# Attention probabilities turned two key tiles at a time: two PSUM banks taken in one run of eight transposes, and split one behind the other

## The chip, the core and the metric

The kernel runs on one core of one Trainium2 chip. A core has five engines with a queue of instructions each: TensorE (PE, matrix products, with the loading of its stationary operand shown apart as PEld), VectorE (DVE), ScalarE (ACT), GpSimd (POOL) and SyncE (SP, which only issues transfers here). They work side by side and wait for one another through semaphores. TensorE writes its results to PSUM, in banks of 2 KB for each of 128 partitions, which VectorE and ScalarE read. The metric is the device time of one execution in microseconds, the median over the runs.

## What is computed

One step of a one-layer streaming encoder on 2048 prompt rows and 64 sample rows of width 1024. One input projection feeds a convolution branch and a banded attention; both are gated, merged, projected, and followed by a feed-forward part. Cut to what matters here:

```python
def conv_module(u, hist, w_dw, b_dw, ln_g, ln_b, w_out):
    ext = jnp.concatenate([hist, u], axis=1)
    y = lax.conv_general_dilated(ext, w_dw[:, None, :], ...)      # 31 taps, 512 channels
    y = jax.nn.silu(layer_norm(y + b_dw, ln_g, ln_b))
    return y @ w_out, ext[:, -(CONV_K - 1):]

def band_attend(q, k, v, q_pos, k_pos, rel_bias):
    s = jnp.einsum('bqhd,bkhd->bhqk', q, k) * ATTN_SCALE
    s = s + rel_bias[:, rel][None]
    s = jnp.where(mask, s, NEG_INF)      # own chunk of 64 and the 8 chunks before it
    p = jax.nn.softmax(s, axis=-1)
    return jnp.einsum('bhqk,bkhd->bqhd', p, v)

def encoder_layer(x, c, conv_hist, attend, p):
    h = rms_norm(x, p['norm1_g']) * (1 + sc1) + sh1
    glu_a, glu_b, q, k, v, g_conv, g_attn = jnp.split(h @ p['w_in'], offs, axis=-1)
    conv_out, conv_state = conv_module(glu_a * jax.nn.sigmoid(glu_b), conv_hist, ...)
    q = rms_norm(q.reshape(B, T, N_HEADS, HEAD_DIM), p['q_norm_g'])
    k = rms_norm(k.reshape(B, T, N_HEADS, HEAD_DIM), p['k_norm_g'])
    attn_out = attend(q, k, v, p['rel_bias']).reshape(B, T, ATTN_DIM) @ p['w_attn_out']
    merged = jax.nn.sigmoid(g_conv) * conv_out + jax.nn.sigmoid(g_attn) * attn_out
    x = x + gt1 * (merged @ p['w_o'])
    h2 = rms_norm(x, p['norm2_g']) * (1 + sc2) + sh2
    gate, up = jnp.split(h2 @ p['w_ffn_in'], 2, axis=-1)
    x = x + gt2 * ((jax.nn.silu(gate) * up) @ p['w_ffn_out'])
    return x, conv_state, k, v
```

There are 8 heads of 64 channels. All data are 32-bit floats.

## The kernel before

**Numbers.** A 32-bit operand is split into a high and a low part that TensorE can take at speed. `split` (L725) is one copy on ScalarE, which makes the high part, and one subtraction on VectorE behind it, which makes the low part, the residue. A product of two split operands is three matmuls (`mm3`, L706). Weights are split in the same way on arrival: `whi` on ScalarE, `wlo` on VectorE or GpSimd.

**Stages.** The rows are cut into four blocks (`PBLOCKS`, L35): block 0 has the 64 sample rows and 512 prompt rows, blocks 1 to 3 have 512 each. For each block the order of stages is q, 0, k, 1, v, 2, 3, g (`ORDER`, L559). q, k and v are the three attention projections (`qkv`, L1200), 0 to 3 are the four channel tiles of the convolution's gated input, each followed by 31 taps on VectorE (`convolve`, L1267), and g is the 16 column tiles of the two gates (`gates`, L1347; with the activation `gate` on ScalarE and a store from ScalarE's queue). The rows of the following block are normalised meanwhile (`norm_tile`, L1172): squares and sums on ScalarE, a power on GpSimd for the reciprocal root, `x_t` on VectorE, and eight transposes on TensorE (`pt<-ident,x_t`). When all four blocks are through, a second phase (from L1692, with PSUM pools of its own) does the merge, the output projection and the feed-forward part.

**The order of the work.** The kernel writes one list of instructions by hand. `Meter` (L85) passes each engine call on and books an estimate of its time to a load per engine in `Stream` (L170); all calls go through one line, so every instruction of the profile says L102 and tiles are told apart by their names. The projections and gates are the main thread. After about each 500 ns of TensorE work by the estimate, `tick` (L211) first does what is due and then gives each `Lane` (L108) a turn. A lane holds generators; a turn runs one of them from one `yield` to the next, and a yielded time says when it may go on by TensorE's estimated clock. The lanes are, in order, `norm_lane` (normalisation), `work` (rows of queries and keys, `qk_rows` L1064), `attn` (attention, at most two heads at a time), `tail` (`conv_norm`, L1289) and `conv` (the taps). `attn` has turns at least `ATTN_NS` = 600 ns apart and none while VectorE's load is over 3000 ns or ScalarE's over 4000 ns ahead of TensorE's (L1608); in block 3 the spacing is 0 and a turn takes two steps. What is left when the last block's gates are through is run out by `attn.drain` (L1684). A scheduler then places the instructions of that list on the engines' queues, where their order is fixed.

**Attention.** `attend(i)` (L1495) is one head of one block. In block 0, heads of the prompt rows and of the sample rows ("s") alternate, and a query tile looks back at up to four key tiles; in the other blocks a query tile has 640 keys (five key tiles). Per head:

- For each of the four query tiles: the score products (`sc<-kk,q`) into the one score tile of PSUM; then `softmax_max` (L1382), which is one VectorE instruction (adds the bias and takes the maximum, `pr<-sc,bias`) and one on ScalarE (exponential and sum, `pr<-pr,sm`); then, a tile late, `softmax_scale` (L1398), a reciprocal on VectorE and a scaling, on ScalarE for every head (`ON_ACT` names all). A tap waits in the order for the last such maximum (`ahead_of_taps`).
- Then for each key tile `jj` in `seq` (L1574 on): up to four transposes `ptp<-ident,pr` into one general PSUM bank, `split` into `ph` and `pl` (three buffers each), a `yield`. The value products `av(jj)` (L1562), which accumulate `po<-ph,vv` and `po<-pl,vv` in the one bank "o", wait in the list `pend` until three key tiles are split, and run before the fourth is turned. The generator yields with a time for each value product, and without one after each key tile.
- Then `finish_head` (L1432): two halves of `po` are added (`o_p` for the prompt rows), and every second head is split and stored.

The general banks are five (`ps_g`, tag "gp", L771); projections, gates, normalisation, the means of the convolution (`pm<-s,ones`) and the transposed probabilities all take them in turn. Two banks hold one tile of scores and one holds `po`, which makes eight in all.

**The convolution's normalisation.** `conv_norm` (L1289) begins when all taps of a block are done: GpSimd adds the four channel tiles to `s`, TensorE multiplies by ones for the mean (first `pm`), VectorE subtracts it, ScalarE squares, GpSimd adds the squares, TensorE multiplies by ones again (second `pm`), and the rest follows on ScalarE, VectorE and GpSimd. In block 0 it is done twice, for the sample rows and for the prompt rows.

Of the kernel before, what the change touches and what calls it, by code (L numbers as in the profile page):

```python
# [8 lines left out]
F32 = mybir.dt.float32  # L9
# [7 lines left out]
P = 128  # L17
# [600 lines left out]
def streaming_layer(ctx: ExitStack, tc: tile.TileContext, I, O):  # L618
    nc = tc.nc
    stream = Stream()  # L620
    pe, dve, act, gps = (
        Meter(e, n, stream) for e, n in ((nc.tensor, "pe"), (nc.vector, "dve"), (nc.scalar, "act"), (nc.gpsimd, "pool"))
    )
# [28 lines left out]
    ident = const.tile([P, P], F32, name="ident")  # L652
# [72 lines left out]
    def split(hi, lo, src):  # L725
        act.activation(hi, src, AF.Copy)
        stream.after("dve", "act")
        dve.tensor_tensor(lo, src, hi.bitcast(F32), ALU.subtract)
# [42 lines left out]
    ps_g = p1.enter_context(tc.tile_pool(name="ps_g", bufs=5, space=PSUM))  # L771
# [626 lines left out]
    def softmax_scale(pr, sm, n, w, on_act):  # L1398
        dve.reciprocal(sm[:n, 3:4], sm[:n, 2:3])
        if on_act:  # L1400
            stream.after("act", "dve")
            act.activation(pr[:n, :w], pr[:n, :w], AF.Copy, scale=sm[:n, 3:4])
        else:
            dve.tensor_scalar(pr[:n, :w], pr[:n, :w], sm[:n, 3:4], None, ALU.mult)
# [48 lines left out]
    def spans(b):  # L1453

        if b == "s":
            return 0, SMP, 0, CACHE + SMP
        past = QB if b else 0
        return SMP + QB * b, QB, CACHE + SMP + QB * b - past, QB + past
# [18 lines left out]
    def fetch_qk(i):  # L1477
        if i < len(order) and ("qk", i) not in now:
            x, h = order[i]
            now["qk", i] = load_qk(x, h, *spans(x))  # L1480

    def fetch(i):
        if i < len(order) and i not in loaded:
            x, h = order[i]
            fetch_qk(i)
            if now["bias"] is None or now["bias"][0] != h:
                now["bias"] = h, load_bias(h)
            loaded[i] = stream.load["pe"] + DMA_LAG

    def fetch_v(i):  # L1490
        if i < len(order) and ("v", i) not in now:
            x, h = order[i]
            now["v", i] = load_v(h, *spans(x)[2:])

    def attend(i):  # L1495
        x, h = order[i]
        q0, nq, k0, nk = spans(x)
        yield lambda: now["scored"] == i - 1
        fetch(i)
        fetch_v(i)  # L1500
        if not i:
            fetch_qk(1)
        yield loaded[i]
        (q2, kk), (_, bias), vnow = now["qk", i], now["bias"], now["v", i]
        tiles = []
        for t in range(0, nq, P):
            n = min(P, nq - t)
            if x not in (0, "s"):
                ps = ps_a.tile([P, 2, 512], F32, tag="s", name="sc")
                for j in range(2):  # L1510
                    for d in range(2):
                        pe.matmul(ps[:, j, :320], q2[:, d, t : t + P], kk[:, t + 320 * j : t + 320 * j + 320], start=d == 0, stop=d == 1)
                w, src, bs = 640, ps[:, :, :320], bias[:, ::-1]
            else:
                w = nk if x == "s" else t + P

                if "banks" not in now:
                    sc = ps_a.tile([P, 2, 512], F32, tag="s", name="sc")
                    now["banks"] = [sc[:, 0:1], sc[:, 1:2]]
                ps = now["banks"].pop(0)  # L1520
                now["banks"].append(ps)
                for d in range(2):
                    pe.matmul(ps[:n, 0, :w], q2[:, d, t : t + n], kk[:, :w], start=d == 0, stop=d == 1)
                src, bs = ps[:n, 0:1, :w], bias[:n, 64:384][:, ::-1] if x == "s" else bias[:, :w][:, ::-1]
            pr, sm, free, ready = softmax_max(src, n, w, bs)
            tiles.append((pr, sm, n, w))
            if t + P < nq:
                yield free + PE_LAG, SCORE_ROOM
            else:
                fetch(i + 1)  # L1530
                if (x, order[min(i + 2, len(order) - 1)][0]) in ((0, 0), ("s", "s")):
                    fetch_qk(i + 2)
                now["scored"] = i
            if t:
                softmax_scale(*tiles[-2], x in ON_ACT)
        yield ready
        softmax_scale(*tiles[-1], x in ON_ACT)
        yield stream.when("act" if x in ON_ACT else "dve") + PE_LAG
        while now["finished"] < i - 1:
            yield lambda: now["finished"] == i - 1  # L1540
        fetch_v(i + 1)
        po = ps_a.tile([P, 512], F32, tag="o", name="po")
        if x == "s":
            pt = ps_g.tile([P, 512], F32, tag="gp", name="ptp")
            ph = wk.tile([P, 512], F32R, tag="ph", name="ph", bufs=3)
            pl = wk.tile([P, 512], F32R, tag="pl", name="pl", bufs=3)
            js = ((0, P), (1, P), (2, SMP))
            for j, m in js:
                c = slice(j * SMP, j * SMP + SMP)
                pe.transpose(pt[:m, c], tiles[0][0][:SMP, j * P : j * P + m], ident[:SMP, :SMP])  # L1550
            stream.after("act", "pe")
            split(ph[:, : 2 * SMP], pl[:, : 2 * SMP], pt[:, : 2 * SMP])
            split(ph[:SMP, 2 * SMP : 3 * SMP], pl[:SMP, 2 * SMP : 3 * SMP], pt[:SMP, 2 * SMP : 3 * SMP])
            yield stream.when("dve") + PE_LAG
            for j, m in js:
                c = slice(j * SMP, j * SMP + SMP)
                for y_ in (ph, pl):
                    pe.matmul(po[:, :SMP], vnow[:m, j], y_[:m, c], start=j == 0 and y_ is ph, stop=j == 2 and y_ is pl)
        else:
            seq = (0, 1, 2, 3) if x == 0 else (3, 4, 0, 1, 2)  # L1560

            def av(jj, ph, pl, _):  # L1562
                if x:
                    uses = [(jj, 0, min(jj, 3) + 1)] + ([(jj + 5, jj + 1, 4)] if jj < 3 else [])
                else:
                    uses = [(jj, jj, 4)]
                for j, a, e in uses:
                    for y_ in (ph, pl):
                        pe.matmul(
                            po[:, a * P : e * P], vnow[:, j], y_[:, a * P : e * P], start=jj == seq[0] and y_ is ph,  # L1570
                            stop=jj == seq[-1] and y_ is pl and j == uses[-1][0], skip_group_check=True,
                        )

            pend = []  # L1574
            for jj in seq:
                if len(pend) > 2:
                    yield pend[0][3] + PE_LAG
                    av(*pend.pop(0))
                pt = ps_g.tile([P, 512], F32, tag="gp", name="ptp")
                t0 = 0 if x else jj  # L1580
                for t in range(t0, 4):
                    j = (jj - t + (5 if t > jj else 0)) if x else jj
                    pe.transpose(pt[:, t * P : t * P + P], tiles[t][0][:, j * P : j * P + P], ident)
                ph = wk.tile([P, 512], F32R, tag="ph", name="ph", bufs=3)
                pl = wk.tile([P, 512], F32R, tag="pl", name="pl", bufs=3)
                stream.after("act", "pe")
                w = 512 - t0 * P
                if x in ON_POOL and jj % 2:
                    p32 = temp("p32")
                    act.activation(p32[:, :w], pt[:, t0 * P :], AF.Copy)  # L1590
                    act.activation(ph[:, t0 * P :], p32[:, :w], AF.Copy)
                    stream.after("pool", "act")
                    gps.tensor_tensor(pl[:, t0 * P :], p32[:, :w], ph[:, t0 * P :].bitcast(F32), ALU.subtract)
                    pend.append((jj, ph, pl, stream.when("pool")))
                else:
                    split(ph[:, t0 * P :], pl[:, t0 * P :], pt[:, t0 * P :])
                    pend.append((jj, ph, pl, stream.when("dve")))
                yield
            for args in pend:
                yield args[3] + PE_LAG  # L1600
                av(*args)
        yield stream.when("pe")
        yield from finish_head(h, po, SMP if x == "s" else QB, q0, "s" if x == "s" else "p")
        now["finished"] = i
# [87 lines left out]
    ps_g = ctx.enter_context(tc.tile_pool(name="ps_c", bufs=4, space=PSUM))  # L1692
# [184 lines left out]
    for s, (lo, hi) in enumerate(CBLOCKS):  # L1877
        tiles = token_tiles(lo, hi)
# [476 lines left out]
```

## Time and profile before

| | |
|---|---|
| Median of 3 runs | 2961.91 us (2960.33 to 2962.21) |
| The profiled execution | 2958.2 us, with a span of 2956.1 us |
| Mean granted TensorE clock | 0.996 |
| TensorE busy before the first attention | 158.48 of 173.00 us |
| TensorE busy from the first attention to the end of the first phase | 987.41 of 1017.00 us (173 to 1190) |
| TensorE busy behind it | 1749.66 of 1766.00 us |

The span runs from the first instruction to the last. The attention's own groups of instructions, with their count, busy time and mean:

| Engine, instruction | count | busy us | mean ns |
|---|---|---|---|
| TensorE, scores `sc<-kk,q` | 448 | 91.1 | 320 |
| TensorE, turned probabilities `ptp<-ident,pr` | 584 | 89.9 | 272 |
| TensorE, values `po<-ph,vv` and `po<-pl,vv` | 248 each | 75.1 each | 313, 320 |
| ScalarE, exponential and scaling `pr<-pr,sm` | 272 | 200.2 | 747 |
| ScalarE, copy `ph<-ptp` | 168 | 87.2 | 533 |
| VectorE, maximum `pr<-sc,bias` | 136 | 97.9 | 720 |
| VectorE, residue `pl<-ptp,ph` | 168 | 100.0 | 606 |

Busy means that an instruction was in execution; a TensorE that waits for an operand between two matmuls is idle. A matmul's own duration overlaps those of its neighbours (272 ns for a transpose is from its start to its modelled end), so its price in time is read from the distance of starts. In a row of a timeline, the columns are start and duration in us, engine, line, operation, output and inputs by name, sizes, and how many such instructions stand in a run; a bracket gives the idle time in front and what ended it. In a table of windows each engine has its busy time and, in brackets, the number of its instructions, and then follow the granted clock of TensorE as a share of the full one, the busy share of the transfer engines, and GB/s.

### The profile page before, as it was taken

To read this page: it belongs to the slowest core of one execution; us is meant where nothing else is said; L and a number is where in the kernel's file an instruction comes from. 1 tells how busy PE (TensorE), PEld (TensorE's weight loads), DVE (VectorE), ACT (ScalarE), POOL (GpSimd) and SP (SyncE) were. 2 spreads that over 40 slices of the span, in tenths; PEclk is the share of its full clock that TensorE was granted. 3 is DMA by queue.
4 is the path that set the end of the run, shared out by engine and by line. 5 is a ranking of instruction groups with operands and counts; after the bars stand their busy time and mean duration, and the time that the engine had idled before them with its cause. 6 is when DMAs were issued, how large, how long until landed. Compare 5 with 4: busy or idle time off the path is not lost.

```text
span 2956.1 us, 44848 instructions
## 1 busy us (share of the span) xinstructions
PE 2895.5 (98%) x16193; PEld 2587.1 (88%) x16193; DVE 2041.9 (69%) x3648; ACT 1363.3 (46%) x2453; POOL 1166.4 (39%) x753
## 2 busy tenths in 40 slices
PE   8999899999999999999999999999999999999999
PEld 5899777787888788888999998999999999999998
DVE  5897687668857885577777746676666547566666
ACT  3345633661465257464433345444444345444442
POOL 1101310111011103454566452366667742465767
PEclk9999999999999999999999999999999999999999
DMA  9988889988987889985444776332333965333333
GB/s 320 320 291 293 285 277 299 286 260 275 303 277 221 277 248 286 280 293 172 150 152 146 261 256 228 99 118 93 114 122 104 332 223 185 97 96 111 115 107 126
DMA packets 467066, 628.04 MB, mean 212 GB/s; under 512 B 36196, under 2 KB 314584, under 8 KB 466845
## 3 DMA queue, kind: packets, MB, share of 16 engines
q1 hardware_dynamic: 452944, 606.11, 63.1%
q10 hardware_dynamic: 13901, 19.08, 1.8%
q8 instruction: 127, 2.08, 0.3%
q14 instruction: 94, 0.77, 0.1%
HBM read 476.53 MB, written 148.54 MB: 211 GB/s over the span
## 4 chain that ended last, share of the span: by engine, by line
PE 48%; DVE 2%; ACT 1%; issue 1%; DMA 0%; POOL 0%; ACTq 0%; DVEq 0%
PE ps L102 29%; PE pd L102 14%; PE pw L102 5%; DVE wlo L102 1%; DVE pw L102 0%; ACT whi L102 0%; DVE ps L102 0%; DVE t L102 0%; DMA tg<-g_d 0%; DVE sums L102 0%; PE pt L102 0%; DVE acc L102 0%; ACT xn L102 0%; DVE hid L102 0%; ACT hid L102 0%
## 5 line engine op out<-in xcount | busy, mean ns | idle before, releaser
L102 PE MATMUL ps<-t,whi 128*128 128x384 f32 (+1 forms) x2112 | 501.7, 322 | 3.0 <-DVE u L102 0.9
L102 POOL TENSOR_TENSOR wlo<-wst,whi 128x1024 fp32r<-128x1024 f32 (+1 forms) x159 | 363.7, 2298 | 243.3 <-ACT whi L102 231.0
L102 ACT ACTIVATE whi<-wst 128x1024 fp32r<-128x1024 f32 (+1 forms) x265 | 258.3, 979 | 321.8 <-PE ps L102 135.0
L102 PE MATMUL ps<-b,whi 128*128 128x384 f32 (+1 forms) x1584 | 381.6, 326 | 6.4 <-ACT early L102 2.7
L102 PEld LDWEIGHTS ps<-t,whi 128*128 128x128 f32 x2112 | 367.7, 188 | 10.2 <-ACT u L102 3.3
L102 DVE SCALAR_TENSOR_TENSOR y<-u,wd,y 128x512 f32<-128x512 f32 (+1 forms) x480 | 369.3, 773 | 6.3
L102 PE MATMUL ps<-hh,whi 128*128 128x512 f32 (+2 forms) x992 | 361.6, 365 | 0.0
L102 DVE TENSOR_TENSOR acc<-acc,pd 128x512 f32<-128x512 f32 x482 | 322.2, 684 | 48.5 <-PE pd L102 46.0
L102 PE MATMUL ps<-hl,whi 128*128 128x512 f32 (+2 forms) x992 | 345.6, 348 | 0.0
L102 PE MATMUL ps<-hh,wlo 128*128 128x512 f32 (+2 forms) x992 | 345.1, 348 | 0.0
L102 PE MATMUL ps<-t,wlo 128*128 128x384 f32 (+1 forms) x1056 | 338.2, 321 | 0.0
L102 PE MATMUL pd<-whi,hid 128*128 128x512 f32 x912 | 297.2, 391 | 0.3 <-DVE hid L102 0.3
L102 PEld LDWEIGHTS ps<-b,whi 128*128 128x128 f32 x1584 | 278.0, 189 | 14.5 <-ACT early L102 4.1
L102 POOL TENSOR_TENSOR r<-t,mhalf 128x1 f32<-128x1 f32 (+2 forms) x68 | 84.1, 1244 | 444.5 <-DVE t L102 434.2
L102 PE MATMUL ps<-b,wlo 128*128 128x384 f32 (+1 forms) x792 | 256.8, 324 | 0.0
L102 ACT ACTIVATE pr<-pr,sm 128x640 f32<-128x640 f32 (+3 forms) x272 | 200.2, 747 | 111.8 <-DVE sm L102 109.2
L102 PEld LDWEIGHTS ps<-hh,wlo 128*128 128x128 f32 x992 | 186.7, 188 | 21.7
L102 PEld LDWEIGHTS ps<-hh,whi 128*128 128x128 f32 x992 | 187.1, 189 | 18.6 <-issue 1.9
L102 DVE TENSOR_TENSOR wlo<-wst,whi 128x1024 fp32r<-128x1024 f32 (+1 forms) x106 | 135.1, 1277 | 98.7 <-ACT whi L102 97.2
L102 PEld LDWEIGHTS pd<-whi,hid 128*128 128x128 f32 x912 | 171.1, 188 | 36.2 <-ACT hid L102 0.7
L102 PEld LDWEIGHTS ps<-hl,whi 128*128 128x128 f32 x992 | 187.5, 189 | 15.5 <-issue 1.4
L102 PEld LDWEIGHTS ps<-t,wlo 128*128 128x128 f32 x1056 | 198.1, 188 | 0.8
(233 smaller groups left out, 6297.4 us busy)
## 6 DMA issues: line engine op xcount, KB each, us to landing
whi<-w_din_h SPq DMA_DIRECT2D x72, 512.0 KB, 6.7
wlo<-w_din_l SPq DMA_DIRECT2D x72, 512.0 KB, 7.5
wst<-sum_d SPq DMA_DIRECT2D x131, 256.0 KB, 2.9
wfo<-in_w_ffn_out SPq DMA_DIRECT2D x64, 512.0 KB, 4.1
wmod<-in_w_ada SPq DMA_DIRECT2D x46, 512.0 KB, 9.0
sum_d<-ws SPq DMA_DIRECT2D x88, 256.0 KB, 2.0
wst<-in_w_ffn_in SPq DMA_DIRECT2D x85, 256.0 KB, 3.3
wst<-in_w_in SPq DMA_DIRECT2D x40, 512.0 KB, 7.6
```

Source lines behind the costliest of these rows:

```text
L102: self.last = f(*args, **kw)
```

## The change

One new helper, `turn_probs(jj)`, holds the transposes of one key tile. When the loop comes to a key tile that isn't turned yet, it takes that one and the next in `seq` and turns both, eight transposes in a row into two general banks, and notes the two banks in `turned`. The loop then splits the first, comes round without a `yield`, finds the second turned already, and splits it. So the only `yield` without a time left is the one behind the second of a pair, or behind a last one that stands alone. The rule for the value products changes with it: one runs when more than two tiles are in `pend`, or when exactly two are in it and a pair is about to be turned (not for the last key tile of `seq` on its own).

In blocks 1 to 3 with `seq` = (3, 4, 0, 1, 2) the steps of a head were: turn 3, turn 4, turn 0, value 3 and turn 1, value 4 and turn 2, values 0, 1, 2. Now they are: turn 3 and 4, value 3 and turn 0 and 1, value 4 and turn 2, values 0, 1, 2. In block 0 with `seq` = (0, 1, 2, 3): turn 0, turn 1, turn 2, value 0 and turn 3, values 1, 2, 3 become: turn 0 and 1, value 0 and turn 2 and 3, values 1, 2, 3. Key tile `jj` of block 0 has 4 - `jj` transposes, since earlier query tiles don't see it. The sample heads are as they were.

```diff
--- before.py
+++ after.py
@@ -1571,16 +1571,21 @@
                             stop=jj == seq[-1] and y_ is pl and j == uses[-1][0], skip_group_check=True,
                         )
 
-            pend = []
+            def turn_probs(jj):
+                pt = ps_g.tile([P, 512], F32, tag="gp", name="ptp")
+                for t in range(0 if x else jj, 4):
+                    j = (jj - t + (5 if t > jj else 0)) if x else jj
+                    pe.transpose(pt[:, t * P : t * P + P], tiles[t][0][:, j * P : j * P + P], ident)
+                return pt
+
+            pend, turned = [], {}
             for jj in seq:
-                if len(pend) > 2:
+                if len(pend) > 2 or len(pend) == 2 and jj not in turned and jj != seq[-1]:
                     yield pend[0][3] + PE_LAG
                     av(*pend.pop(0))
-                pt = ps_g.tile([P, 512], F32, tag="gp", name="ptp")
-                t0 = 0 if x else jj
-                for t in range(t0, 4):
-                    j = (jj - t + (5 if t > jj else 0)) if x else jj
-                    pe.transpose(pt[:, t * P : t * P + P], tiles[t][0][:, j * P : j * P + P], ident)
+                if jj not in turned:
+                    turned.update({i: turn_probs(i) for i in seq[seq.index(jj) :][:2]})
+                pt, t0 = turned.pop(jj), 0 if x else jj
                 ph = wk.tile([P, 512], F32R, tag="ph", name="ph", bufs=3)
                 pl = wk.tile([P, 512], F32R, tag="pl", name="pl", bufs=3)
                 stream.after("act", "pe")
@@ -1595,7 +1600,8 @@
                 else:
                     split(ph[:, t0 * P :], pl[:, t0 * P :], pt[:, t0 * P :])
                     pend.append((jj, ph, pl, stream.when("dve")))
-                yield
+                if not turned:
+                    yield
             for args in pend:
                 yield args[3] + PE_LAG
                 av(*args)
```

## The prediction

> **What bounds the kernel now.** I read the page first, then the windows by stage, then the waits and the timeline around each wait of TensorE.
>
> ```profile
> span 2956.1 us, 44848 instructions
> PE 2895.5 (98%) x16193; PEld 2587.1 (88%) x16193; DVE 2041.9 (69%) x3648; ACT 1363.3 (46%) x2453; POOL 1166.4 (39%) x753
> ```
>
> TensorE is busy for 98% of the span, so time can only be won or lost in the remaining 60.6 us, or by making its own instructions dearer. The profiled execution took 2958.2 us: the span and 2.1 us around it. The median of the timed runs, 2961.91, lies 3.7 us above; I add that at the end.
>
> Attention runs in four stretches, which the windows separate from the stages without it (columns: stretch; stretch length; then busy time of each engine, granted clock, DMA share).
>
> ```profile
> 173.10:439.90 266.80, 251.31 (x1599) 221.78 (x1598) 206.80 (x449) 141.91 (x322) 51.14 (x43) 0.98 0.87 288
> 468.70:676.30 207.60, 203.21 (x1150) 169.96 (x1148) 148.85 (x307) 117.58 (x217) 21.57 (x21) 0.99 0.87 275
> 742.90:954.60 211.70, 209.01 (x1195) 178.25 (x1194) 152.62 (x313) 118.40 (x217) 21.94 (x22) 1.00 0.84 269
> 1020.60:1186.20 165.60, 163.41 (x871) 138.24 (x869) 122.98 (x234) 105.56 (x185) 24.01 (x16) 1.00 0.88 272
> ```
>
> TensorE idles 15.5, 4.4, 2.7 and 2.2 us there, 24.8 us in all. That is all that a better attention order could win from idling. A worse one has no such limit. VectorE is busy for 72 to 78% of these stretches, in order, and most of it is the convolution taps: whatever stands behind it waits.
>
> **The change part by part.**
>
> *What moves.* Nothing is added or removed: the built order of the changed kernel has the same instructions of each kind on each engine. From the first attention tile to the first merge the order differs on all five queues; behind that TensorE's order is the same, so all that follows costs nothing. Per head of a full block the generator yields 8 times instead of 10, so attention ends some 3 to 12 us of TensorE work earlier in its block.
>
> *The transposes themselves.* Their price is read from starts.
>
> ```profile
> 1030.29 0.39 PE L102 MATMUL ps<-hh,wlo 128*128 128x512 f32 x1
> 1030.52 1.04 PE L102 MATMUL ptp<-ident,pr 128*128 128x128 f32 x8
> 1031.39 0.27 PE L102 MATMUL pt<-ident,u 128*30 128x128 f32 x1
> 1031.42 0.48 PE L102 MATMUL ps<-hh,whi 128*128 128x512 f32 x1
> 1031.74 0.39 PE L102 MATMUL ps<-hl,whi 128*128 128x512 f32 x1
> 1031.97 0.40 PE L102 MATMUL ps<-hh,wlo 128*128 128x512 f32 x1
> 1032.21 0.60 PE L102 MATMUL ptp<-ident,pr 128*128 128x128 f32 x4
> 1032.56 0.48 PE L102 MATMUL ps<-hh,whi 128*128 128x512 f32 x1
> 1032.88 0.40 PE L102 MATMUL ps<-hl,whi 128*128 128x512 f32 x1
> ```
>
> A 512-column product starts 0.23 us after the one before it. From 1030.29 to 1031.74 there are two such steps (0.46) and nine transposes: 0.99 us, 0.110 each. From 1031.97 to 1032.88 there are two and four transposes: 0.45, 0.113 each. A run of eight thus saves about 0.01 us against two of four. The built order has 122 runs of transposes where it had 162 (34 of eight instead of 7): 40 x 0.012 = **0.5 us won**.
>
> *The splits, one behind the other.* The second tile of a pair waits for the first one's copy and residue, and both banks stay taken meanwhile.
>
> ```profile
> L102 ACT ACTIVATE ph<-ptp x168: 210/597/620, 181.1 to 1182.6; 128x512 fp32r<-128x512 f32 x128, 128x128 fp32r<-128x128 f32 x16, 128x384 fp32r<-128x384 f32 x8, 128x256 fp32r<-128x256 f32 x8
> L102 DVE TENSOR_TENSOR pl<-ptp,ph x168: 207/684/693, 181.7 to 1183.5; 128x512 fp32r<-128x512 f32 x128, 128x128 fp32r<-128x128 f32 x16, 128x384 fp32r<-128x384 f32 x8, 128x256 fp32r<-128x256 f32 x8
>   PEld po L102: 2.8, 8
> ```
>
> Uncovered, each of the 64 pairs would delay its second product by one residue: 64 x 0.68 = 44 us. The cover is the projection or gate product that stands between; today only 2.8 us of waits come through. In the built order 53 waits of the value products stand within 2.5 us of their transposes, where 35 did, so I scale: 2.8 x 53/35, **1.4 us lost** (bounds: 0 and 44, taken near the row, since 1 to 2 us of cover were enough in nearly all cases). Of the five general banks I see no new tight wait in the order, and take 0.
>
> *The end of the attention.* In the kernel before the last head's transposes stand bare at the end:
>
> ```profile
> 1180.07 1.20 PE L102 MATMUL ptp<-ident,pr 128*128 128x128 f32 x9 [0.55 <-ACT pr L102]
> 1184.54 0.27 PE L102 MATMUL po<-pl,vv 128*128 128x128 f32 x1
> 1186.21 0.56 PE L102 MATMUL ps<-cin,whi 128*128 128x320 f32 x2 [1.40 <-DVE o_p L102]
> ```
>
> In the changed order twelve gate products stand behind them. The first merge then waits for the last gate's activation, itself behind a weight copy on ScalarE, for about as long as 1.40 less 0.7 of what now overlaps. With the 0.55 in front: **1.3 us won** (bounds 0 and 2).
>
> *Block 1's normalisation.* The longest wait of TensorE is for a normalised row tile, whose squares stand on ScalarE behind the softmax of the head just scored:
>
> ```profile
> 294.80 0.66 PE L102 MATMUL pt<-ident,x_t 128*128 128x128 f32 x4 [1.24 <-DVE x_t L102]
> 337.30 1.16 ACT L102 ACTIVATE pr<-pr,sm 128x512 f32<-128x512 f32 x2
> 338.37 0.61 ACT L102 ACTIVATE junk<-x_t 128x512 f32<-128x512 f32 x1
> 341.83 1.09 PE L102 MATMUL pt<-ident,x_t 128*128 128x128 f32 x4 [5.65 <-DVE x_t L102]
> ```
>
> From the first square to the transposes 3.46 us pass, with ScalarE's share in front of them 2.2. In the changed order that softmax is done earlier and the squares stand nearly first: 5.65 falls to about 3.2, **2.5 us won** (bounds 0 and 5.65). The first such tile's transposes stand 6 us of work later: its 1.24 goes, **1.2 won**.
>
> *The convolution's means.* The mean is a product of ones with a sum made on GpSimd behind the last tap on VectorE.
>
> ```profile
> 535.99 3.11 DVE L102 SCALAR_TENSOR_TENSOR y<-u,wd,y 128x512 f32<-128x512 f32 x4
> 539.25 1.09 POOL L102 TENSOR_TENSOR s<-s,y 128x512 f32<-128x512 f32 x1 [25.00 <-DVE y L102]
> 540.39 1.13 PE L102 MATMUL pm<-s,ones 128*128 128x512 f32 x2 [1.27 <-POOL s L102]
> 548.78 1.12 PE L102 MATMUL pm<-s,ones 128*128 128x512 f32 x2 [0.75 <-POOL s L102]
> L102 POOL TENSOR_TENSOR wlo<-wst,whi 128x1024 fp32r<-128x1024 f32 x9 | 22.0, 2450 | 51.1 <-ACT whi L102 39.0 <-PE po L102 9.5 <-DMA w_din_h<-whi 2.6
> L102 POOL TENSOR_TENSOR s<-s,ln 128x512 f32<-128x512 f32 x12 | 15.6, 1302 | 25.3 <-ACT ln L102 23.6 <-DMA g_d<-gate 1.3
> L102 DVE SCALAR_TENSOR_TENSOR y<-u,wd,y 128x512 f32<-128x512 f32 (+1 forms) x424 | 322.0, 764 | 5.8
> L102 DVE CUSTOM_DVE_ANT_0 pr<-sc,bias 128x640 f32<-128x640 f32 (+5 forms) x136 | 97.9, 720 | 46.7 <-PE sc L102 41.0 <-DMA bias<-rb_d 4.6
> ```
>
> Here attention's earlier steps push the taps back. In block 1 the changed order has, behind a tile's scores, two taps, that tile's maximum and then GpSimd's sum before the mean, with no product of TensorE between: 2 x 0.76 + 0.82 + 1.09 = 3.4 us; the scores ahead of it wait 1.2 more for the maximum before them. Less the 1.27 of today: **3.4 lost** (bounds 0 and 4.6). In block 0 the second mean follows a sum behind a weight residue on GpSimd, with 1.2 us of the residue's 2.45 covered: 1.25 + 1.30, **2.5 lost** (today 3.7 us of work cover it). In block 3 a tap and the sum, 0.76 + 1.09, stand uncovered: **1.7 lost**. Block 1's second mean has 9 us of work in front: its **0.75 is won**.
>
> *The key rows' power.* GpSimd's power instruction holds VectorE, and that the scores:
>
> ```profile
> L102 POOL TENSOR_TENSOR r<-t,mhalf 128x8 f32<-128x8 f32 x24 | 46.1, 1920 | 143.7 <-DVE t L102 139.6 <-DVE sm L102 4.0
> 408.28 0.69 DVE L102 TENSOR_TENSOR kn<-kn,r 128x512 f32<-128x512 f32 x1 [1.81 <-POOL r L102]
> 409.02 0.28 DVE L102 CUSTOM_DVE_ANT_0 pr<-sc,bias 128x128 f32<-128x128 f32 x1
> 409.36 0.50 PE L102 MATMUL sc<-kk,q 128*128 128x256 f32 x2 [2.37 <-DVE sm L102]
> ```
>
> In the changed order the scale clears 6 us earlier: **2.4 won**. The next one now stands in front of the pair's first residue: 1.92 + 0.69 + 0.76 + 0.68 = 4.05, less 1.9 of work: **2.1 lost** (bounds 0 and 4). In block 0, a second score product stands behind two taps and a weight residue on VectorE; about 3 us against 1.9 waited there now: **1.1 lost**.
>
> *The clock after a wait.*
>
> ```profile
> 341.80:346.00 4.20, 4.05 (x12) 3.01 (x13) 4.20 (x12) 1.95 (x4) 2.48 (x1) 0.54 0.89 182
> 409.30:413.00 3.70, 3.64 (x12) 3.11 (x13) 3.16 (x11) 2.25 (x8) 0.00 (x0) 0.66 1.00 297
> 540.30:544.00 3.70, 3.61 (x22) 2.95 (x23) 2.45 (x5) 2.01 (x5) 0.18 (x2) 1.00 0.81 322
> ```
>
> After the 2.37 us wait the granted clock is 0.66 over 3.7 us: 1.3 us lost beside the wait. After 1.27 us it is 1.00. So waits over some 2 us cost 1.3 to 1.9 more. The one at 409 goes (**1.3 won**); its successor (**1.3 lost**), block 1's mean and block 0's (**1.7 each lost**, between 1.3 and 4.2 x 0.46 = 1.9) may fall in. [...]
>
> *The sum.* Won: 0.5 + 1.3 + 2.5 + 1.2 + 0.75 + 2.4 + 1.3 = 9.95. Lost: 1.4 + 3.4 + 2.5 + 1.7 + 2.1 + 1.1 + 1.3 + 1.7 + 1.7 = 16.9. Net 7.0 us slower: 2958.2 + 7.0 = 2965.2 for the profiled execution, + 3.7 = **2969 us** for the runs. The direction rests on waits behind VectorE's order, not on the transposes.
>
> **The rivals.**
>
> *Not slower: the waits only change places.* If VectorE and GpSimd run ahead of where the order puts them, the means wait as they do today (1.3, or 1.6 in block 3) and no new wait is long enough for the clock. Lost then: 1.4 + 0 + 1.3 + 1.6 + 2.1 + 1.1 = 7.5, against 9.95 won: 2961.9 - 2.5 = 2959 us. For it: 75% load leaves VectorE room. Against: the tap rows stand back to back with no idle before the mean.
>
> *Faster: attention's earlier end pays.* If the normalisation's wait goes whole, with its slow clock (5.65 + 1.9), and the 409 wait (3.7), the end (1.9) and the early tiles (1.2 + 0.75 + 0.5), 15.6 us are won; with 6 of new waits left, 2961.9 - 9.6 = 2952 us. Deciding point: whether the tile of 341.83 is loaded and squared before TensorE gets there. Against: 3.46 us of that chain are its own.
>
> *The pairs come apart.* The planner may place the transposes between products as before, and then nothing moves: 2962. The order speaks against it: 34 runs of eight.
>
> **How the numbers follow.** About 0.2% (5.9 us) is what a measurement can tell from no change. The forecast has 0.45, with its own range 2968 to 2984; the waits that only change places 0.30; the faster case 0.18; the pairs apart 0.04; beyond 2984, with the value products' cover gone in part (up to 44), 0.03. Slower then has 0.48, same 0.33 (0.30, 0.04, less what touches a border), faster 0.19. The range of 8 in 10 runs from 2954, short of the faster case's centre, to 2985: the sum with all losses at their bounds (block 1's mean + 1.2, the residue + 1.9, the gains of normalisation - 3.7 and of the end - 1.3, the clock + 1.9, the products + 5: 15 more).
>
> **What would show it.** Right: transposes at 0.11 us each; means waiting 3 us or more in block 1 and over 2 in block 0, with a halved clock behind them; the second long wait at the normalisation shorter than 5.65; the last head covered. Wrong: total idle of the four stretches at 24.8 us or below; value products waiting far over 4 us in all; the projection's first product waiting for a general bank; any difference behind the merge.

## The result and the profile after

The changed kernel takes 2975.98 us (median of 4 runs, 2972.78 to 2978.33), the kernel before 2961.12 us beside it (4 runs, 2959.86 to 2962.21): a ratio of 1.0055, with a 95% interval of 1.0043 to 1.0067, or 14.9 us slower. The profiled execution of the changed kernel is the slowest of its four, 2978.33 us, and that of the kernel before, 2958.2 us, is faster than all four beside it, so the two traces lie 20.0 us apart. First the page of the changed kernel, with the view of the cores (span and mean granted clock) of the two kernels behind it, after first:

```profile
span 2976.1 us, 44869 instructions
PE 2902.7 (98%) x16193; PEld 2591.7 (87%) x16193; DVE 2040.1 (69%) x3648; ACT 1364.2 (46%) x2453; POOL 1162.4 (39%) x753
```

```profile
core 0: 2976.1 us, clock 0.994
```

```profile
core 0: 2956.1 us, clock 0.996
```

The instructions are the same in number on every engine. TensorE is idle for 2976.1 - 2902.7 = 73.4 us where it was idle for 60.6, which is 12.8 more, and its same 16193 instructions are busy for 7.2 us more. Most of that second part is the clock: 0.994 instead of 0.996 means that it was halved for about 2 x 0.006 x 2976 = 36 us instead of 2 x 0.004 x 2956 = 24, and half of these 12 us can be lost by it. VectorE, ScalarE and GpSimd have no more to do than before.

The windows of the four attention stretches of the changed kernel, from the first score product of a block to the last value product (in the last row to the first merge product), with the columns of the prediction's windows:

```profile
174.90:437.10 262.20, 244.17 (x1545) 216.32 (x1543) 194.85 (x431) 139.66 (x319) 46.78 (x43) 0.95 0.86 282
477.90:677.40 199.50, 192.12 (x1073) 161.60 (x1072) 143.96 (x298) 116.92 (x215) 21.69 (x20) 0.99 0.84 269
755.00:961.40 206.40, 201.97 (x1157) 171.97 (x1156) 146.16 (x303) 117.25 (x216) 21.84 (x21) 1.00 0.83 263
1033.70:1201.10 167.40, 164.13 (x872) 137.96 (x870) 120.53 (x235) 106.68 (x185) 22.27 (x16) 1.00 0.83 263
```

Attention itself is through sooner, in block 1 in 199.5 us instead of 207.6, and yet TensorE idles more in less time: 18.0, 7.4, 4.4 and 3.3 us, 33.1 in all against 24.8. VectorE's load is 71 to 74% of these stretches and no higher than before. What changed is where the waits fall. The waits of TensorE between 170 and 1215 us, after (total us, times, longest):

```profile
PE pm L102 <- POOL s L102: 8.6, 5, 3.2
PE sc L102 <- DVE sm L102: 7.1, 9, 1.3
PE ps L102 <- ACT hh L102: 5.1, 1, 5.1
PE po L102 <- DVE pl L102: 3.1, 3, 1.7
PE pt L102 <- ACT part_h L102: 2.2, 1, 2.2
PE ptp L102 <- ACT pr L102: 2.2, 3, 1.0
PE pt L102 <- DVE x_t L102: 1.9, 2, 1.1
```

and the same view of the kernel before:

```profile
PE pt L102 <- DVE x_t L102: 8.2, 3, 5.6
PE sc L102 <- DVE sm L102: 5.7, 5, 2.4
PE pm L102 <- POOL s L102: 5.6, 4, 1.9
PE ps L102 <- DMA whi<-w_dqkv_h: 2.6, 1, 2.6
```

The means wait 3.0 us more, the normalised row tiles (`x_t`) 6.3 less, and in their place a product waits 5.1 us for their split copy (`hh`). The longest new wait, in the timeline of the changed kernel, is the first mean of block 1:

```profile
551.30 0.74 DVE L102 SCALAR_TENSOR_TENSOR y<-u,wd,y 128x512 f32<-128x512 f32 x1
552.07 0.75 DVE L102 SCALAR_TENSOR_TENSOR y<-u,wd,y 128x512 f32<-128x512 f32 x1
552.75 0.82 DVE L102 CUSTOM_DVE_ANT_0 pr<-sc,bias 128x640 f32<-128x640 f32 x1
553.49 0.75 DVE L102 SCALAR_TENSOR_TENSOR y<-u,wd,y 128x512 f32<-128x512 f32 x1
554.27 0.75 DVE L102 SCALAR_TENSOR_TENSOR y<-u,wd,y 128x512 f32<-128x512 f32 x1
554.94 0.82 DVE L102 CUSTOM_DVE_ANT_0 pr<-sc,bias 128x640 f32<-128x640 f32 x1
555.68 0.75 DVE L102 SCALAR_TENSOR_TENSOR y<-u,wd,y 128x512 f32<-128x512 f32 x1
556.57 1.09 POOL L102 TENSOR_TENSOR s<-s,y 128x512 f32<-128x512 f32 x1 [27.00 <-DVE sm L102]
557.72 1.55 PE L102 MATMUL pm<-s,ones 128*128 128x512 f32 x2 [3.25 <-POOL s L102]
```

In the kernel before the last ten taps of the last channel tile ran nearly in a row there, from 530.30 us on, with two residues between them. Now a head is at its scores when the taps end: every two taps a maximum of 0.82 us stands between, the sum on GpSimd (1.09 us) comes behind the last, and TensorE has nothing to do for 3.25 us.

### The profile page after: what moved, and what is told of

It reads as the page before. It is cut to its first block, busy times and chain, and to the rows that moved or that the text cites. A ratio compares the mean times of both kernels' runs of the same rounds, so it can differ in the third digit from the quotient of the medians.

```text
span 2976.1 us, 44869 instructions
## 1 busy us (share of the span) xinstructions
PE 2902.7 (98%) x16193; PEld 2591.7 (87%) x16193; DVE 2040.1 (69%) x3648; ACT 1364.2 (46%) x2453; POOL 1162.4 (39%) x753
```

## The experiments

Twelve kernels were run, each against the kernel before on the same chip; the ratios have 95% intervals. They fall in three questions.

**Is it the pairs or the turns?** The change does two things at once: it turns two key tiles in one go, and it gives a head 8 turns where it had 10, counted from its first turned key tile to its last value product (6 where it had 8 in block 0). Three kernels and a control take them apart.

The first keeps the pairs and yields behind every split, as before:

```diff
-                if not turned:
-                    yield
+                yield
```

> The pairs stay, but the generator yields behind every split again, 10 times per head of a full block as before. Pace theory (the time goes because a head needs 8 turns instead of 10, so its maxima, scalings and splits come sooner and push taps, sums and powers behind them on VectorE and GpSimd): the time comes back to 2961 to 2966, the means wait 6 us or less in all (5.6 before, 8.6 after the change) and the clock is halved for 24 us or less (20 before, 34 after). Pair theory (two banks held at once, the second split behind the first, cost the time): 2972 to 2978, with value products waiting 3 us or more. Order theory (any order other than that of before loses as much, whatever moved it): 2968 to 2980, with waits at places of its own.

Measured: 2963.49 us against 2958.50, 1.0017 (1.0009 to 1.0026). Two thirds of the loss are gone, with the pairs in place, and the means wait 2.9 us. The value products wait 0.5 us in all. The clock is halved for 30.7 us, counted as in the expectation, and not for 24 or less: that sign of the pace theory did not come. A third of the loss, 5 us, stays.

The second keeps the 8 turns, and turns each key tile right before its own split:

```diff
-                    turned.update({i: turn_probs(i) for i in seq[seq.index(jj) :][:2]})
-                pt, t0 = turned.pop(jj), 0 if x else jj
+                    turned.update({i: None for i in seq[seq.index(jj) :][:2]})
+                turned.pop(jj)
+                pt, t0 = turn_probs(jj), 0 if x else jj
```

> The turns are left out as in the change (8 per head), but each key tile is turned right before its own split, as before. Pace theory: 2970 to 2978, the means wait 7 to 10 us. Pair theory: 2961 plus or minus 3. Order theory: 2968 to 2980.

Measured: 2974.34 us, 1.0054 (1.0042 to 1.0066): the whole loss. It shows less than it was meant to, for with nothing between the two splits of a turn the two sets of transposes stand in a row on TensorE all the same. But the waits are other ones:

```profile
PE sc L102 <- DVE sm L102: 12.3, 13, 4.3
PE pm L102 <- POOL s L102: 5.1, 4, 3.2
PE pt L102 <- DVE u L102: 2.7, 1, 2.7
```

The means wait 5.1 us, less than in the kernel before and less than the 7 to 10 of the pace theory, and the scores 12.3. The same loss is made up of other waits.

The third tells apart what the first two leave mixed: both tiles of a pair are split in one turn, and the turn that the change leaves out is given back behind them.

```diff
                 if not turned:
-                    yield
+                    yield from [None] * (1 + seq.index(jj) % 2)
```

> The changed kernel with the turn that it leaves out given back behind the pair: both tiles of a pair are still turned and split in one turn, but two turns pass behind them, so a head takes 10 turns as before. All kernels with 8 turns in every block but one gave 13 to 20 us more than before, all with 10 turns 5 or less. Pace theory (the number of turns of a head decides): 2958 to 2966 against 2959. Burst theory (two copies and two residues in one turn stand in front of other work on ScalarE and VectorE): 2970 to 2978. In between, 2966 to 2970, would leave both in.

Measured: 2964.40 us against 2958.29, 1.0020 (1.0010 to 1.0030). The burst of two splits costs no more, within the intervals, than splits in turns of their own (1.0017); the missing turns do. The control lets the kernel before give its turns closer together (`ATTN_NS` 480 in place of 600). In the traces that moves TensorE's order in block 0 alone (1091 places of its queue, against 3668 in the changed kernel), and block 0's attention takes 266.5 us where it took 267.2:

> The kernel before with turns of the attention allowed 480 ns apart in place of 600: no pairing, all 10 turns. Since a turn is only given after whole products (0.64 to 0.72 us of estimated work for most), few turns move. Pace theory and pair theory: 2958 to 2965. Order theory: 2966 to 2978, for the order differs in a good part of the attention's stretch.

Measured: 2959.75 us, 0.9999 (0.9990 to 1.0008). So not every other order loses; in that form the order theory falls. The control says nothing of other orders in blocks 1 to 3.

**Where is it lost?** Pairs and left-out turns in some blocks alone, by a condition on the block in the loop (`two = x == 0`, `x != 0`, `x == 1`):

```diff
-            pend, turned = [], {}
+            pend, turned, two = [], {}, x == 0
...
-                if len(pend) > 2 or len(pend) == 2 and jj not in turned and jj != seq[-1]:
+                if len(pend) > 2 or two and len(pend) == 2 and jj not in turned and jj != seq[-1]:
...
-                    turned.update({i: turn_probs(i) for i in seq[seq.index(jj) :][:2]})
+                    turned.update({i: turn_probs(i) for i in seq[seq.index(jj) :][: 1 + two]})
```

> Pairs and left-out turns for the prompt heads of block 0 alone; blocks 1 to 3 as before. In the changed kernel the distance to the kernel before grew by about 8 us over block 0, 2 over block 1, 1 to 2 over block 2 and 3 to 4 over block 3. Pace theory: 2961 + 8 = 2969, with the second mean of block 0 waiting 2 us or more and the clock halved about 20 us before 360 us. Pair theory: a quarter of the loss or less, 2961 to 2965, since block 0 has 4 key tiles and narrow ones. Order theory: anything from 2961 to 2976, and the blocks' parts do not add up to 15.

> Pairs and left-out turns in blocks 1 to 3, block 0 as before. With block 0 alone 5 us were lost of some 15. If the blocks' losses add up, 10 us here, 2968 to 2970 against 2958.5; the first mean of block 1 waits 3.2 us with a halved clock behind it. If each order has losses of its own, the parts do not add up: 2961 to 2965 or over 2973.

> Pairs and left-out turns in block 1 alone. My step: the first mean there waits 3.2 us where it waited 1.27, the clock is halved for 3.4 us behind it (1.7 lost), the second mean no longer waits (0.75 won), and a score at about 660 waits 1.2: about 4 us slower, 2961 to 2965. Rival (block 1 is not where the loss is; its waits are given back by the earlier end of the attention): within 2 us of before.

Measured: block 0 alone 1.0018 (1.0009 to 1.0027), 5.0 us; blocks 1 to 3 1.0050 (1.0037 to 1.0062), 13.6 us; block 1 alone 1.0019 (1.0010 to 1.0028), 4.5 us. Every block in which it was tried by itself loses, and block 1 by about what its step said: its trace has the same wait of 3.25 us for the first mean. Block 0 lost 2963.51 - 2958.50 = 5.0 us, short of the 8 of the pace theory and inside the range of the pair theory, so this run does not tell the two apart; blocks 1 to 3, with 2972.32 us, fell between the two ranges of their expectation. The parts add up to 5.0 + 13.6 = 18.6 us, more than the 14.9 of the whole but within its interval, which ends at 0.0067 x 2961 = 19.8 us, so whether they add up is not shown either way. Blocks 2 and 3 were not run by themselves.

**Which waits are it?** If the waits of the means are the loss, making the means due later should bring it back:

```diff
-PE_LAG = 400.0
+PE_LAG, MEAN_LAG = 400.0, 3400.0
...
-        yield stream.when("pool") + PE_LAG
+        yield stream.when("pool") + MEAN_LAG
         pm = total()
```

(at both means), in the changed kernel and in the kernel before:

> The changed kernel, with both products for the convolution's means due 3 us later by the stream's clock (the lag behind GpSimd 3400 ns in place of 400). Wait theory (the waits of the means, 8.6 us after the change, and the halved clock behind them at 326 and 558 us are the loss): the means wait 2 us or less in all, and of the 15 us 8 to 12 come back: 2962 to 2967. Rival (the waits only move to what stands behind the means, the rows of the next block or the merge): 2970 to 2978, with as much idle time in all, 34 to 40 us between 160 and 1216.

> The same lag in the kernel before, where the means wait 5.6 us. Wait theory: 4 to 6 us faster than before, about 2954. Rival: within 3 us of before, or slower, for the normalisation of the convolution ends later and its steps move among the attention's.

Measured: in the changed kernel 2963.67 us, 1.0018 (1.0009 to 1.0027): two thirds of the loss come back, as the wait theory said; in the kernel before 2961.37 us, 1.0010 (1.0001 to 1.0018), slower instead of 4 to 6 us faster. In both the means hardly wait any more (0.6 and 1.3 us), but in the kernel before another wait came up in their place, for the first row tile of the next block (5.17 us at 298.89, where it was 1.24):

```profile
PE pt L102 <- DVE x_t L102: 10.8, 2, 5.6
```

The second place is the block's boundary. Three row tiles in normalisation at a time in place of two:

```diff
-NORM_W = 2
+NORM_W = 3
```

> The kernel before, with three row tiles of the next block in normalisation at a time in place of two (the fourth tile then starts before the third is through). Every run so far has TensorE waiting 5 to 7.6 us there, at the last row tile of block 1, with the clock halved for 6.8 to 10.2 us behind it. Start theory (the fourth tile starts too late, whatever the attention does): the wait falls to 2 us or less and the clock is halved for 3.4 us or less, 5 to 8 us faster than before. Rival (its chain through ScalarE and VectorE, behind the attention's work, is the limit): 4 us of wait or more remain, within 3 us of before.

> The same in the changed kernel. Start theory: 5 to 8 us faster than the changed kernel, about 2967 where the kernel before has 2959; the means' waits, some 8 us, stay. Rival: 2972 to 2978, as the changed kernel.

> Both remedies in the changed kernel: three row tiles in normalisation and the means due 3 us later. If the means and the block's boundary are the two places of the loss, they add up: 5 us above before with the later means alone, less 5 to 8: 2953 to 2960, not slower than before. If what is taken away comes back elsewhere: 2962 to 2970.

Measured: in the kernel before 2961.05 us, 1.0006 (0.9997 to 1.0015), with a wait of 5.25 us left at the boundary, as the rival had it. In the changed kernel 2973.39 us, 1.0053 (1.0039 to 1.0067): here the wait did fall, to 2.49 us, and the time did not, since a score product waits 4.99 us a little later (408.56 us). With both remedies 2979.20 us, 1.0067 (1.0053 to 1.0081), the highest ratio of all (its interval overlaps that of the changed kernel), although its means wait 0.7 us in all. The row tile at the boundary, which three tiles alone had brought down to 2.49 us, waits 5.8 again:

```profile
PE sc L102 <- DVE sm L102: 13.1, 14, 1.7
PE pt L102 <- DVE x_t L102: 5.8, 1, 5.8
PE pt L102 <- DVE h L102: 3.2, 1, 3.2
PE pt L102 <- DVE u L102: 2.8, 1, 2.8
...
PE pm L102 <- POOL s L102: 0.7, 2, 0.4
```

So the wait theory falls in its strong form: the gain of the later means was that of one order, and not the price of those waits. What goes with the time in all runs but one (the changed kernel with later means) is the number of turns. The table adds two stretches of each trace, from the first score product to the first merge product and from there to the end of the span; each is one execution.

| | turns in a full block | ratio to the kernel before | first score to first merge, us | from there to the end, us |
|---|---|---|---|---|
| before | 10 | 1 | 1013.2 | 1769.9 |
| before with spacing 480, with later means, with three row tiles | 10 | 0.9999, 1.0010, 1.0006 | 1012.4, 1012.1, 1016.5 | 1768.7, 1774.8, 1770.1 |
| pairs with 10 turns (first and third kernel) | 10 | 1.0017, 1.0020 | 1016.8, 1017.3 | 1774.0, 1775.3 |
| pairs, and two turns left out, in block 0 alone, in block 1 alone | 10, but 8 in block 1 of the second | 1.0018, 1.0019 | 1015.9, 1016.3 | 1768.1, 1770.5 |
| 8 turns in blocks 1 to 3 | 8 | 1.0050 | 1023.7 | 1772.0 |
| 8 turns in all: as changed, single, three row tiles, both remedies | 8 | 1.0055, 1.0054, 1.0053, 1.0067 | 1026.1, 1023.8, 1022.6, 1023.6 | 1775.1, 1772.1, 1774.1, 1774.5 |
| 8 turns in all, later means | 8 | 1.0018 | 1012.2 | 1774.7 |

The first stretch goes with the turns, again but for later means; the second does not. In the nine kernels with 1772.0 us or more in the second stretch, TensorE's products stand in another order than in the kernel before for up to some 220 places behind the first merge product; in the four others they stand as before, and the stretch takes 1768.1 to 1770.5 us. So 2 to 5 us of many of these losses lie behind the attention. By the traces they are the whole loss of the kernel before with later means, and the whole loss that is left with them in the changed kernel, whose first stretch is back at 1012.2 us.

No run was faster than the kernel before by more than its interval.

## Why the prediction was right in direction and small in size

It forecast 2969 us for what became 2976, inside its range of 2968 to 2984, with 7.1 us lost where 14.9 were. The direction came from the mechanism that it named, waits behind VectorE's changed order. The total owes something to luck: some terms were too large and others too small, and a stretch that it put at nothing lost 5.2 us.

- **What moves.** Attention's stretch is shorter by 4.6, 8.1 and 5.3 us in blocks 0 to 2 (prediction: 3 to 12), and nothing but order changed. That the pace is what costs the larger part is shown by the third kernel of the first question: given its turns back, the kernel loses 6.1 us instead of 14.9.
- **The transposes** cost what the step said. In the changed kernel's timeline a product starts at 1045.02, eight transposes follow, and the second product behind them starts at 1046.36; less two steps of 0.23 this is 0.88 us, 0.110 each:

```profile
1045.02 0.40 PE L102 MATMUL ps<-hh,wlo 128*128 128x512 f32 x1
1045.25 1.04 PE L102 MATMUL ptp<-ident,pr 128*128 128x128 f32 x8
1046.05 0.47 PE L102 MATMUL ps<-hh,whi 128*128 128x512 f32 x1
1046.36 0.39 PE L102 MATMUL ps<-hl,whi 128*128 128x512 f32 x1
```

- **The means.** The step named the right places. Block 0's second mean waits 2.37 us behind the weight residue on GpSimd (2.5 lost by the step), block 3's 1.40 (1.7), block 1's second no longer waits (0.75 won). Block 1's first was a little too large: 3.25 us and 0.66 for the score in front of it, less the 1.27 of before, make 2.6 where the step had 3.4. In block 0 the second score and the mean behind it wait 1.32 and 0.70 us at 262, against the 1.91 of one mean before: 0.1 lost, where the step had 1.1. The mean of block 2 waits 0.92 where it waited 1.64; the prediction took that 1.64 for one of block 3, whose means wait for nothing in the kernel before.
- **The key rows' power.** The wait of 2.37 us for the score is gone as said. Behind the power now waits the first product of a residue (0.95 us at 427.04), where the step had 2.1. The run of transposes ahead of it (0.97 at 424.03) waits for a scaling on ScalarE, and not for the power.
- **The value products** wait 3.1 us themselves, in three places, where 1.4 more was forecast: 2.8 more than the 0.3 us of before. One of the three is the 0.95 at 427.04 again. The cover held nearly everywhere; a cost of the two banks is not to be seen in the waits.
- **The end.** The first merge waits 1.3 us for the last gate's activation, as said, and the bare transposes (0.55) are gone; 0.65 of 1.95 us are won, half of the term.
- **Block 1's normalisation** is a step that failed: 3.7 us won by the sum, 1.2 in the trace (the waits for its tiles are 7.0 us, 1.9 and 5.1, where they were 8.2), and the long wait did not shrink. The transposes of the last tiles wait 0.84 and no longer 5.65 us, but the product behind them waits for the split copy instead:

```profile
344.18 1.10 PE L102 MATMUL pt<-ident,x_t 128*128 128x128 f32 x8 [0.84 <-DVE x_t L102]
346.21 0.41 PE L102 MATMUL sc<-kk,q 128*128 128x128 f32 x2 [0.94 <-DMA kk<-k_d]
348.26 0.75 DVE L102 TENSOR_SCALAR x_t<-x_t,r 128x1024 f32<-128x1024 f32 x1 [0.66 <-POOL r L102]
348.93 0.68 DVE L102 TENSOR_REDUCE ssq<-sq 128x8 f32<-128x512 f32 x1
349.91 1.68 DVE L102 TENSOR_SCALAR h<-pt,A,B 128x128 f32<-128x128 f32 x5
350.99 0.63 ACT L102 ACTIVATE hh<-h 128x512 fp32r<-128x512 f32 x1 [1.85 <-DVE h L102]
351.67 0.80 PE L102 MATMUL ps<-whi,hh 128*128 128x512 f32 x1 [5.06 <-ACT hh L102]
```

  The eight transposes were done at 345.3. Before VectorE reads them, from 349.52 on, its queue has the work of the next row tile, whose squares it waits for on ScalarE (1.85 us, to 347.25) and whose power on GpSimd (0.66), then that tile's `x_t` (0.75) and the sum of a tile's squares (0.68). The step followed the chain to the transposes and not on to the next operation that VectorE has in its queue.
- **The clock** was sized too low: 3.4 us by the sum, net. Between 170 and 1400 us it is halved for 34.1 us where it was for 20.5; TensorE is busy in these stretches for 27.7 and 17.1 us, and half of the difference, 5.3, is lost by estimate (from 559.92 to 561.20 us in the last of the three windows below, at 0.50, a 512-column product starts 0.43 us after the one before it, and 0.23 at the full clock). (The rest of the 7.2 us of busy time is not traced.) The step charged only waits of over 2 us each. The windows of three halved stretches of the changed kernel:

```profile
326.10:332.90 6.80, 5.73 (x13) 4.02 (x14) 1.50 (x6) 5.19 (x9) 1.02 (x1) 0.51 0.83 275
346.70:356.90 10.20, 5.23 (x18) 4.50 (x19) 8.89 (x23) 5.49 (x12) 2.20 (x2) 0.50 0.71 234
558.30:561.70 3.40, 3.40 (x9) 2.29 (x8) 2.39 (x4) 1.67 (x3) 0.36 (x1) 0.50 1.03 226
```

  The second of them was 6.8 us long in the kernel before. Here two short waits, 0.84 and 0.94, stand ahead of the long one, and the clock is down before the long one ends its first us; the step had left out every wait as short as these.
- **Not foreseen:** a score product at 659.62 (1.18 us), value products at 953.24 (1.67), and that the three waits for weights near 990 us, 3.5 us in all, would give way to one of 2.25 for a transpose behind VectorE's taps. (There the view names ScalarE's `part_h`, which itself waits for VectorE behind four taps.)
- **Behind the merge** a step failed: it put nothing there, because TensorE's order was to be the same. In the traces it is another, from 144 to some 220 products behind the first merge product. From there to the end the changed kernel takes 5.2 us more; in the first 45 us TensorE waits 3.1 us, where it waited 0.5:

```profile
1214.68 0.53 PE L102 MATMUL ps<-cin,whi 128*128 128x320 f32 x2 [0.73 <-DVE m L102]
1217.45 0.56 PE L102 MATMUL ps<-cin,whi 128*128 128x320 f32 x2 [0.77 <-DVE t L102]
1225.98 0.49 DVE L102 SCALAR_TENSOR_TENSOR t<-tg,ps 128x320 f32<-128x320 f32 x1 [2.48 <-DMA tg<-g_d]
1226.53 0.56 PE L102 MATMUL ps<-cin,whi 128*128 128x320 f32 x2 [1.53 <-DVE t L102]
```

  VectorE waits here for stored gates to come back (`tg<-g_d`). The last of these waits stands as 1.47 and 1.53 us in the kernels with 8 turns in blocks 1 to 3 and with three row tiles too, so it is no accident of one execution; why the order changes so late is open. Of the 20.0 us between the two traces 1.9 lie ahead of the first score product, where nothing was changed, 13.0 from there to the first merge product, and 5.2 behind it. Of the four signs of being wrong this one came; the idle time of the four stretches (33.1 us) and the waits of the value products (3.1) did not show theirs, and no wait of a projection for a bank is to be seen.

Of the rivals, the waits that only change places came nearest to one truth: single waits do move, and taking one away moves it on. But their sum is larger with 8 turns. TensorE's idle time, the span less its busy time on the page, is 67.9 to 73.4 us in five of the six kernels with 8 turns in all of blocks 1 to 3 (61.7 in the one with later means), and 59.5 to 65.7 in the six with 10 turns; the kernels with pairs in block 0 alone and in block 1 alone have 68.0 and 65.2. Why the sum grows is not settled. VectorE is not busier in the attention's stretches, and no one wait carries the loss; that a head with fewer turns leaves less work of TensorE between its own dependent steps is argued from the way the order is written, and was not measured by itself. What the pairs cost with 10 turns, 5 to 6 us, lies by the two traces in part before the first merge product (3.6 and 4.2 us) and in part behind it (4.1 and 5.4); some of it may be the order alone, as the control with later means lost 2.7 us without pairs.

## What to carry to other kernels

Where an order is written in turns, putting two steps in one turn is a change of pace, and it is this that has to be priced: count the turns, and give the lost one back to see which of the two matters. Where an engine is busy for 98%, as here, look at what stands behind a wait before you count its end as a gain: two remedies that each shortened their own waits when tried alone gave the highest ratio when put together. Compare the order and the time of the stretches behind the change too; here a stretch taken to be the same lost 5 us. Here the halved clock went with the idle time in a step of 3.41 us and not with single waits (next section), so price it by that.

## What the hardware showed that was not expected

In the traces of the kernel before and of the changed kernel, the granted clock changes in steps of 3.41 us. Between 170 and 1400 us the stretches at half clock last 3.41, 6.83 or 10.24 us, and the full-clock stretches between two of them are whole multiples of 3.413 us too (64.85, 58.03, 518.83 and 300.37 us in the kernel before, which are 19, 17, 152 and 88 steps). Whether a halved stretch followed a wait went with how the wait fell into these steps. The same wait of the same order shows it, in the kernel before and in the kernel with pairs in block 1, whose order is the same up to there. The kernel before:

```profile
257.26 0.43 PE L102 MATMUL pm<-s,ones 128*128 128x64 f32 x2 [1.91 <-POOL s L102]
```

```profile
257.20:261.20 4.00, 3.94 (x30) 3.68 (x30) 0.77 (x5) 0.81 (x4) 0.80 (x4) 1.00 0.75 166
```

The kernel with pairs in block 1:

```profile
258.10:262.10 4.00, 3.92 (x18) 3.93 (x19) 0.78 (x5) 0.55 (x3) 0.82 (x4) 0.57 0.61 171
```

It waits 1.91 us as well, at 258.18, and runs 18 matmuls in 4 us instead of 30. In the first trace a step ends within the wait, at 256.90 us (24 steps before the next halved stretch, which starts at 338.82), so that 1.55 us of the wait fall into one step and 0.36 into the next. In the second the wait falls whole into one step, and the clock is halved at its end, at 258.61 (0.57 over the window of 4.00 us is 3.4 us at half clock). With the traces of all 14 kernels cut into these steps between 170 and 1220 us, the step behind one with 1.9 us of idle time or more was halved in 44 cases of 44, with 1.35 to 1.9 us in 24 of 55, and with 0.5 to 1.35 us in none of 189 (counting full-clock steps, idle time as the sum of the gaps between matmuls); the kernel before and the changed kernel by themselves have 5 of 5, 5 of 8 and none of 30. How the waits fall into the steps may also be part of why runs of one kernel differ (the kernel before took 2952.83 to 2965.78 us in 29 runs on one chip); that was not tested.
